# Early gate/up products over three weight blocks instead of two, with the third block's weight rows in an h block tile

## The chip, the core and the metric

The kernel runs on one core of a Trainium2 chip. Its time is the device time of one execution in microseconds (us). The names of the engines are TensorE (PE in the profile; PEld is its weight load), VectorE (DVE), ScalarE (ACT), GpSimd (POOL) and SyncE (SP, which here only issues transfers). Each engine works through its own list of instructions in the order in which the program holds them.

## The reference

One encoder layer on 1024 tokens of width 1024: a gated feed-forward network (FFN), a mixer, a second FFN, a last norm.

```python
def _swiglu(x, w_gate, w_up, w_down):
    return (jax.nn.silu(x @ w_gate) * (x @ w_up)) @ w_down
...
        h = _rmsnorm(x, ffn1_norm[l])
        x = x + 0.5 * _swiglu(h, ffn1_w_gate[l], ffn1_w_up[l], ffn1_w_down[l])
        h = _rmsnorm(x, mix_norm[l])
        z = h @ w_in[l]
...
        x = x + jnp.concatenate([y_a, y_b], axis=-1) @ w_out[l]
        h = _rmsnorm(x, ffn2_norm[l])
        x = x + 0.5 * _swiglu(h, ffn2_w_gate[l], ffn2_w_up[l], ffn2_w_down[l])
    return _rmsnorm(x, final_norm)
```

The inner width of an FFN is 2816, which is 22 column blocks of 128 for gate and 22 for up.

## The kernel before

**Products.** The change lies in `gate_up`, which computes gate and up of one FFN. It multiplies in the Winograd form of Strassen's scheme: a 2x2 arrangement of blocks takes seven products instead of eight. A block `b` is one pair of weight columns of gate (`g`) or of up (`u`); there are 22, in the order g, u, g, u. Each block has seven products, M = 1 to 7. Product M multiplies a weight block, or a sum of weight blocks, with one of seven token blocks: A11, A12, A22, which are parts of the normed input h, and S1 to S4, which are sums and differences of such parts (`A_OF`: 1 uses A11, 2 A12, 5 S1, 6 S2, 3 S4, 7 S3, 4 A22). Every operand is split into a high and a low half in a short float format (`split`: ScalarE casts the high half, VectorE subtracts to get the low half), and a product is high times high, high times low and low times high (`mm3`, L137 to L139) over four slices k: 12 matmuls of 128x128 by 512 columns.

**Tiles.** The high and low halves of the seven token blocks are 14 tiles of pool `big`, which holds 14 (`h_units`; A11h is the high half, A11l the low one). A block's weights arrive as two rows of 512 KB (`row`, L288; r0 holds the quarters for M 1 and 2, r1 the others, and in M 5, 6, 7 and 4 VectorE overwrites quarters with their differences, L299, L302, L305, L308). Rows take one of five buffers of pool `raw`; a split weight (`wu`) takes one of eight buffers of pool `unit`, which the product that reads it gives back.

**The start of an FFN.** A11 and A12 are made first. The other token blocks are made by `kinds`: s1 (norms of the second half of the tokens, L233, sums, L249, and S1's split), s2 (L254), s4 (L259), s3 (L264), a22 (a split only). `STAGES` says behind which step each is written in the program. The steps of before are: M 1 and M 2 for blocks 0, 1, 2; then 5, 6, 3, 7, 4 for blocks 0 and 1 in turn; then 5, 6, 3, 7 of block 2; and from block 3 on one block after the other, M 1 of the block, M 4 of the block ahead of it, M 2, 5, 6, 3, 7. Weights are written six steps ahead (`ahead=6`), and the evacuations of the first six steps wait for step 6 (`hold=6`): product 6, 7 and 4 add to the PSUM bank of product 1 (X), so the copy `m1` must have left the bank before product 6 writes it. A scheduler orders each engine's instructions from this program; the order is what the section on the change shows.

`gate_up` runs twice, for the first FFN from the start and for the second from about 1045 us.

Of the kernel before, what the change touches and what calls it, by code (L numbers as in the profile page):

```python
# [10 lines left out]
F32 = mybir.dt.float32  # L11
# [6 lines left out]
P = 128  # L18
D = 1024
S = 1024  # L20
T = 512
# [25 lines left out]
A_OF = {1: "A11", 2: "A12", 3: "S4", 4: "A22", 5: "S1", 6: "S2", 7: "S3"}  # L47
UNITS = ("A11", "A12", "A22", "S1", "S2", "S3", "S4")
GROUPS = ((0, 4), (4, 8), (8, 11))
STAGES = (5, 5, 6, 8, 9)  # L50


class Net:
# [219 lines left out]
    def gate_up(self, n):  # L273
        nc, d = self.nc, self.d
        self.actd = {
            (u, g): self.dp.tile([q1 - q0, P, T], F32, name=f"act{n}{u}{g}")
            for u in UNITS
            for g, (q0, q1) in enumerate(GROUPS)
        }
        blocks = [(p, m) for p in range(NP) for m in ("g", "u")]  # L280
        rows, sil, fence = {}, {}, {}
        early = 3

        def row(b, i):
            p, m = blocks[b]
            if (b, i) not in rows:
                rows[b, i] = self.rp.tile([P, 2, T], F32, tag="r", name=f"r{m}{i}")
                nc.sync.dma_start(rows[b, i].rearrange("p a t -> p (a t)"), d[f"{m}{n}"][2 * p + i])  # L288
            return rows[b, i]

        def weight(b, M):
            r0 = row(b, 0)
            if M in (1, 2):
                src = r0[:, M - 1]
            else:
                r1 = row(b, 1)
                if M == 5:
                    src = r1[:, 0]
                    nc.vector.tensor_sub(src, r1[:, 0], r0[:, 0])  # L299
                elif M == 6:  # L300
                    src = r1[:, 0]
                    nc.vector.tensor_sub(src, r1[:, 1], r1[:, 0])  # L302
                elif M == 7:
                    src = r0[:, 0]
                    nc.vector.tensor_sub(src, r1[:, 0], r0[:, 0])  # L305
                elif M == 4:
                    src = r0[:, 1]
                    nc.vector.tensor_sub(src, r0[:, 1], r1[:, 0])  # L308
                else:
                    src = r1[:, 1]  # L310
            w = self.unit("wu")
            name = self.split(w[:, 0], w[:, 1], src, after=fence.get("early"))
            if (b, M) == (early - 1, 2):
                fence["early"] = name
            return w

        bank, part = {}, {}
        place = {1: "X", 6: "X", 7: "X", 4: "X", 5: "Z", 3: "Z", 2: "W"}

        def product(b, M, w):  # L320
            ch = place[M]
            new = M in (1, 2, 5)
            if new:
                bank[b, ch] = self.fpsum("p" + ch)
            ps = bank[b, ch]
            hh, hl = self.h[A_OF[M]]
            ins = self.mm3(
                ps, [(w[:, 0, k * P : k * P + P], w[:, 1, k * P : k * P + P], hh[:, k], hl[:, k]) for k in range(4)], start=new
            )
            self.last_mm = ins.ins.name  # L330
            if (b, M) == (len(blocks) - 1, 1):
                self.gate = self.last_mm

        def evac(b, M):
            p, m = blocks[b]
            ps = bank[b, place[M]]
            key = {1: "m1", 5: "m5", 6: "u2"}.get(M)
            if key:
                part[b, key] = self.tmp(key)
                nc.scalar.copy(part[b, key], ps)  # L340
                return
            if M == 4:
                if m == "g":
                    s = self.tmp("s21")
                    self.table(s, ps, AF.Silu)
                    sil[p, "A21"] = s
                else:
                    s = sil[p, "A21"]
                    nc.vector.tensor_mul(s, ps, s)
                    finish(p)  # L350
                return
            key, name = {2: ("m1", "A11"), 3: ("u2", "A12"), 7: ("m5", "A22")}[M]
            t = part.pop((b, key))
            nc.vector.tensor_add(t, ps, t)
            if m == "g":
                self.table(t, t, AF.Silu)
                sil[p, name] = t
            else:
                s = sil[p, name]
                nc.vector.tensor_mul(s, t, s)  # L360
                store(p, name, s)

        def store(p, u, t):
            g = next(i for i, (q0, q1) in enumerate(GROUPS) if q0 <= p < q1)
            nc.sync.dma_start(self.actd[u, g][p - GROUPS[g][0]], t)

        def finish(p):
            a11, a12, a21, a22 = (sil.pop((p, q)) for q in ("A11", "A12", "A21", "A22"))
            s1 = a21
            nc.vector.tensor_add(s1, a21, a22)  # L370
            store(p, "S1", s1)
            s2, s3, s4 = (self.tmp(q) for q in ("S2", "S3", "S4"))
            nc.vector.tensor_sub(s2, s1, a11)
            store(p, "S2", s2)
            nc.vector.tensor_sub(s3, a22, s2)
            store(p, "S3", s3)
            nc.vector.tensor_sub(s4, a12, s2)
            store(p, "S4", s4)

        steps = [(b, M) for M in (1, 2) for b in range(early)]  # L380
        steps += [(b, M) for M in (5, 6, 3, 7, 4) for b in range(early - 1)]
        steps += [(early - 1, M) for M in (5, 6, 3, 7)]
        for b in range(early, len(blocks)):
            steps += [(b, 1), (b - 1, 4)] + [(b, M) for M in (2, 5, 6, 3, 7)]
        steps.append((len(blocks) - 1, 4))
        return steps, weight, product, evac
# [524 lines left out]
def layer(ctx, tc, d):  # L911
# [17 lines left out]
    with ExitStack() as f1:  # L929
# [6 lines left out]
        r[1] = net.rsqrt(ps)  # L936
        net.run(*net.gate_up(1), ahead=6, hold=6, stages=list(zip(STAGES, kinds)))

# [44 lines left out]
    with ExitStack() as f2:  # L983
# [6 lines left out]

        stages = [(1, stats2)] + list(zip(STAGES, h2[1]))
        net.run(*net.gate_up(2), ahead=6, hold=6, stages=stages)
# [85 lines left out]
```

## Time and profile before

| | |
|---|---|
| median of three runs | 1708.3 us (1707.48 to 1708.93) |
| the profiled execution | 1708.28 us, of which the span 1706.5 us |
| TensorE busy | 1655.5 us, 97% of the span |
| VectorE busy | 1111.5 us, 65% |
| ScalarE busy | 679.4 us, 40% |

The profile covers the span; 1.8 us of the execution lie around it. TensorE is busy nearly everywhere, so what is to be read are the stretches in which it is not, or in which its granted clock is below 1.00. A row of the timeline gives the start, the length, and in brackets the time that the engine stood idle ahead of it and what ended that. Matmuls and vector instructions overlap their neighbours, so the pace is read from start to start, not from the length.

### The profile page before, as it was taken

What the parts mean: (1) busy time and instruction counts of PE and PEld (TensorE: products, weight loads), DVE (VectorE), ACT (ScalarE), POOL (GpSimd) and SP (SyncE); (2) the same over time, 40 slices, a digit from 0 to 9 for tenths busy, and PEclk for the clock granted to TensorE, in tenths of its full rate; (3) what the DMA queues carried; (4) which work ended last, traced back from release to release, by engine and by line L of the source; (5) the groups of instructions that cost most, each with busy time, mean ns of one, the idle gap of its engine ahead of it and who ended that gap; (6) DMA issues with size and microseconds to landing.
All of it is one profiled execution on the core that took longest, in us unless ns stands there. A gap on an engine that the chain in (4) does not pass through costs nothing.

```text
span 1706.5 us, 19863 instructions
## 1 busy us (share of the span) xinstructions
PE 1655.5 (97%) x7314; PEld 1345.9 (79%) x7314; DVE 1111.5 (65%) x1771; ACT 679.4 (40%) x1155; POOL 60.3 (4%) x79
## 2 busy tenths in 40 slices
PE   6899999999999999999999999899999999999997
PEld 3688888888888877888877887688888888888875
DVE  7976556565569668852626538966666666579584
ACT  5633333333444445531423324533333333444452
POOL 0000000000000000110304300000000000000000
PEclk9999999999999999999999999999999999999999
DMA  4243232232695332230310342232323332793331
GB/s 161 70 141 100 98 105 99 96 108 75 239 331 188 117 112 74 74 88 19 98 46 13 117 142 86 88 123 93 105 99 105 105 111 75 257 319 133 108 121 50
DMA packets 95697, 200.07 MB, mean 117 GB/s; under 512 B 10472, under 2 KB 14568, under 8 KB 95600
## 3 DMA queue, kind: packets, MB, share of 16 engines
q1 hardware_dynamic: 89104, 187.21, 32.7%
q10 hardware_dynamic: 6496, 11.60, 1.9%
q8 instruction: 57, 0.93, 0.2%
q14 instruction: 40, 0.33, 0.1%
HBM read 145.78 MB, written 52.99 MB: 116 GB/s over the span
## 4 chain that ended last, share of the span: by engine, by line
PE 91%; DVE 7%; ACT 1%; DMA 0%; issue 0%; SPq 0%; DVEq 0%; ACTq 0%
PE pX L137 14%; PE pX L139 14%; PE pX L138 14%; PE pZ L138 7%; PE pZ L137 7%; PE pZ L139 7%; PE pW L139 3%; PE pW L138 3%; PE pW L137 3%; PE pg L139 3%; PE pg L137 3%; PE pg L138 3%; PE pt L583 2%; PE pt L582 2%; PE pt L584 2%; DVE x L233 1%
## 5 line engine op out<-in xcount | busy, mean ns | idle before, releaser
L206 ACT CAST au<-as 128x512 fp32r<-128x512 f32 x154 | 95.9, 623 | 208.7 <-PE pX L139 102.7
L209 DVE TENSOR_TENSOR au<-as,au 128x512 fp32r<-128x512 f32 x154 | 106.1, 689 | 107.7 <-ACT au L206 107.4
L209 DVE TENSOR_TENSOR wu<-rg,wu 128x512 fp32r<-128x512 f32 x154 | 106.1, 690 | 101.4 <-ACT wu L206 101.0
L206 ACT CAST wu<-ru 128x512 fp32r<-128x512 f32 x154 | 95.8, 622 | 155.3 <-PE pX L139 68.4
L209 DVE TENSOR_TENSOR wu<-ru,wu 128x512 fp32r<-128x512 f32 x154 | 105.7, 688 | 57.6 <-ACT wu L206 57.1
L137 PE MATMUL pX<-au,wu 128*128 128x512 f32 x352 | 137.2, 390 | 0.0
L138 PE MATMUL pX<-au,wu 128*128 128x512 f32 x352 | 137.0, 389 | 0.0
L139 PE MATMUL pX<-au,wu 128*128 128x512 f32 x352 | 136.9, 389 | 0.0
L206 ACT CAST wu<-rg 128x512 fp32r<-128x512 f32 x154 | 95.1, 621 | 103.1 <-issue 53.1
L209 DVE TENSOR_TENSOR wu<-wq,wu 128x512 fp32r<-128x512 f32 x154 | 105.2, 685 | 4.2 <-ACT wu L206 4.2
L206 ACT CAST wu<-wq 128x512 fp32r<-128x512 f32 x154 | 94.4, 616 | 8.3 <-PE pX L139 4.2
L137 PEld LDWEIGHTS pX<-au,wu 128*128 128x128 f32 x352 | 66.1, 188 | 14.4 <-ACT wu L206 0.7
L139 PEld LDWEIGHTS pX<-au,wu 128*128 128x128 f32 x352 | 66.1, 188 | 13.8
L138 PEld LDWEIGHTS pX<-au,wu 128*128 128x128 f32 x352 | 66.1, 188 | 13.6
L137 PE MATMUL pX<-A11h,wu 128*128 128x512 f32 x176 | 70.3, 400 | 4.6 <-ACT wu L206 3.4
L139 PE MATMUL pX<-A11h,wu 128*128 128x512 f32 x176 | 70.3, 400 | 3.9 <-DVE wu L209 3.9
L137 PE MATMUL pZ<-S1h,wu 128*128 128x512 f32 x176 | 68.1, 394 | 5.0 <-ACT wu L206 4.7
L138 PE MATMUL pZ<-S1l,wu 128*128 128x512 f32 x176 | 69.3, 394 | 2.6 <-DVE S1l L209 2.5
L137 PE MATMUL pX<-S3h,wu 128*128 128x512 f32 x176 | 68.9, 395 | 2.8 <-ACT S3h L206 2.8
L138 PE MATMUL pX<-A11l,wu 128*128 128x512 f32 x176 | 70.3, 399 | 0.2 <-DVE A11l L209 0.2
L137 PE MATMUL pX<-S2h,wu 128*128 128x512 f32 x176 | 68.6, 390 | 1.9 <-ACT m L340 1.9
L137 PE MATMUL pX<-A22h,wu 128*128 128x512 f32 x176 | 69.7, 396 | 0.0
(255 smaller groups left out, 4125.4 us busy)
## 6 DMA issues: line engine op xcount, KB each, us to landing
rg<-g SPq DMA_DIRECT2D x44, 512.0 KB, 3.5
ru<-u SPq DMA_DIRECT2D x44, 512.0 KB, 3.5
wq<-d SPq DMA_DIRECT2D x88, 256.0 KB, 5.4
x<-x SPq DMA_DIRECT2D x64, 256.0 KB, 5.3
as<-act1S SPq DMA_DIRECT2D x44, 256.0 KB, 3.6
as<-act2S SPq DMA_DIRECT2D x44, 256.0 KB, 3.2
act1S<-S SPq DMA_DIRECT2D x33, 256.0 KB, 2.1
as<-act1A SPq DMA_DIRECT2D x33, 256.0 KB, 4.9
```

Source lines behind the costliest of these rows:

```text
L137: nc.tensor.matmul(out, wh, hh, start=start and i == 0, stop=False, skip_group_check=True)
L138: nc.tensor.matmul(out, wh, hl, start=False, stop=False, skip_group_check=True)
L139: ins = nc.tensor.matmul(out, wl, hh, start=False, stop=stop and i == n - 1, skip_group_check=True)
L206: cast = nc.scalar.copy(hi, src)
L209: (eng or nc.vector).tensor_sub(lo, src, hi.bitcast(F32))
L233: nc.vector.scalar_tensor_tensor(x, x, g, r[c], op0=ALU.mult, op1=ALU.mult)
L582: nc.tensor.matmul(ps, hh, wh, start=k == 0, stop=False)
L583: nc.tensor.matmul(ps, hh, wl, start=False, stop=False)
L584: nc.tensor.matmul(ps, hl, wh, start=False, stop=k == KT - 1)
```

## The change

The third block (`early - 1`, block 2) takes part in all early rounds: the steps are 5, 6, 3, 7, 4 for blocks 0, 1 and 2 in turn, without the last (M 4 of block 2, which stands behind M 1 of block 3 as before). `STAGES` moves with the longer rounds. The two rows of block 2 no longer take buffers of pool `raw`; they share one tile of pool `big`.

```diff
-STAGES = (5, 5, 6, 8, 9)
+STAGES = (5, 5, 7, 10, 12)
...
-        rows, sil, fence = {}, {}, {}
+        rows, sil, fence, extra = {}, {}, {}, []
         early = 3
 
         def row(b, i):
             p, m = blocks[b]
             if (b, i) not in rows:
-                rows[b, i] = self.rp.tile([P, 2, T], F32, tag="r", name=f"r{m}{i}")
+                if b == early - 1:
+                    if not extra:
+                        extra.append(self.big.tile([P, 4, T], F32, tag="b", name=f"r{m}"))
+                    rows[b, i] = extra[0][:, 2 * i : 2 * i + 2]
+                else:
+                    rows[b, i] = self.rp.tile([P, 2, T], F32, tag="r", name=f"r{m}{i}")
...
         steps = [(b, M) for M in (1, 2) for b in range(early)]
-        steps += [(b, M) for M in (5, 6, 3, 7, 4) for b in range(early - 1)]
-        steps += [(early - 1, M) for M in (5, 6, 3, 7)]
+        steps += [(b, M) for M in (5, 6, 3, 7, 4) for b in range(early)][:-1]
```

All 14 tiles of `big` already hold a token block, so the shared tile comes to lie where A22l, the low half of A22, is put later: A22l is written when block 2's rows have been read for the last time. The numbers of matmuls, vector instructions, casts and transfers stay as they are; only their order at the start of the two FFNs differs, and line numbers behind the new lines are 4 or 5 higher.

ScalarE at the first FFN, where S1 is cast (`wu_373` and `wu_376` are the weights of the twelfth step; `x10` to `x13` are tokens of the second half). Before:

```order
L206 CAST wu_341<-ru1_304 128x512
L206 CAST wu_373<-ru1_304 128x512
L206 CAST S1h_187<-x10_118 128x512
L206 CAST S1h_187<-x11_120 128x512
L206 CAST S1h_187<-x12_122 128x512
```

With the change:

```order
L206 CAST wu_359<-ru1_304 128x512
L206 CAST wu_376<-rg_258 128x512
L206 CAST wu_426<-rg1_285 128x512
L206 CAST wu_457<-ru1_304 128x512
L206 CAST S1h_187<-x10_118 128x512
L206 CAST S1h_187<-x11_120 128x512
```

Two more weight casts, those of steps 13 and 14 (M 3 of blocks 0 and 1), stand ahead of S1's casts.

VectorE at the first FFN, where A22l is written (`wu_516` is M 4's weight of block 1; `rg_541` is the second row of block 2). Before:

```order
L308 TENSOR_TENSOR ru0_253<-ru0_253,ru1_304 128x512
L209 TENSOR_TENSOR S3l_192<-x13_124,S3h_191 128x512
L209 TENSOR_TENSOR A22l_186<-x14_126,A22h_185 128x512
L209 TENSOR_TENSOR wu_516<-ru0_253,wu_516 128x512
L209 TENSOR_TENSOR A22l_186<-x15_128,A22h_185 128x512
L209 TENSOR_TENSOR A22l_186<-x16_130,A22h_185 128x512
L209 TENSOR_TENSOR A22l_186<-x17_132,A22h_185 128x512
L354 TENSOR_TENSOR u2_483<-pZ_408,u2_483 128x512
L299 TENSOR_TENSOR rg1_541<-rg1_541,rg0_258 128x512
```

With the change (`rg_258` is the tile with both rows of block 2; `wu_635` is block 2's M 4, the last that reads it):

```order
L313 TENSOR_TENSOR rg_258<-rg_258 128x512
L359 TENSOR_TENSOR m5_455<-pX_291,m5_455 128x512
L209 TENSOR_TENSOR wu_653<-ru0_615,wu_653 128x512
L209 TENSOR_TENSOR wu_635<-rg_258,wu_635 128x512
L365 TENSOR_TENSOR m5_424<-m5_455,m5_424 128x512
L209 TENSOR_TENSOR A22l_186<-x14_126,A22h_185 128x512
L209 TENSOR_TENSOR A22l_186<-x15_128,A22h_185 128x512
```

A22l no longer follows S3l at once; block 2's weights come between them, `wu_635` as the last. Counted in the whole list, the first A22l row stands 50 rows behind the last S1l row here, against 34 before; in the second FFN 47 against 30.

TensorE at the first FFN, from S3 to A22 (`wu_544` is M 5's weight of block 2, `wu_486` M 4's of block 0). Before:

```order
L138 MATMUL pX_291<-S3l_192,wu_468 128x512
L139 MATMUL pX_291<-S3h_191,wu_468 128x512
L137 MATMUL pZ_649<-S1h_187,wu_544 128x512
L138 MATMUL pZ_649<-S1l_188,wu_544 128x512
L137 MATMUL pX_272<-A22h_185,wu_486 128x512
L138 MATMUL pX_272<-A22l_186,wu_486 128x512
L139 MATMUL pX_272<-A22h_185,wu_486 128x512
```

With the change (`wu_553` is M 7's weight of block 2, `wu_617` M 1's of block 3):

```order
L138 MATMUL pX_310<-S3l_192,wu_553 128x512
L139 MATMUL pX_310<-S3h_191,wu_553 128x512
L137 MATMUL pX_272<-A22h_185,wu_571 128x512
L137 MATMUL pX_291<-A22h_185,wu_598 128x512
L137 MATMUL pX_721<-A11h_181,wu_617 128x512
L138 MATMUL pX_721<-A11l_182,wu_617 128x512
L139 MATMUL pX_721<-A11h_181,wu_617 128x512
L138 MATMUL pX_272<-A22l_186,wu_571 128x512
```

Block 2's S1, S2, S4 and S3 products now lie ahead of A22, one in each round, and no weight of block 2 stands between S3 and A22.

## Rows read from the trace of the kernel before

**Rows 1.** The page: busy time of TensorE, and the last chain by engine.

```profile
PE 1655.5 (97%) x7314; PEld 1345.9 (79%) x7314; DVE 1111.5 (65%) x1771; ACT 679.4 (40%) x1155; POOL 60.3 (4%) x79
...
PE 91%; DVE 7%; ACT 1%; DMA 0%; issue 0%; SPq 0%; DVEq 0%; ACTq 0%
```

**Rows 2.** Busy time by stretch, first FFN (columns in the first row).

```profile
core 0: us, PE busy (x) PEld busy (x) DVE busy (x) ACT busy (x) POOL busy (x), PEclk, DMA share, GB/s
...
65.60:77.41 11.81, 7.69 (x25) 5.29 (x24) 11.81 (x21) 7.06 (x13) 0.00 (x0) 0.86 0.65 199
77.41:101.17 23.76, 23.76 (x97) 19.34 (x98) 20.29 (x33) 10.65 (x19) 0.00 (x0) 0.93 0.40 133
```

**Rows 3.** Timeline of TensorE, first FFN.

```profile
45.62 0.39 PE L137 MATMUL pZ<-S1h,wu 128*128 128x512 f32 x1
...
54.58 0.50 PE L137 MATMUL pX<-S2h,wu 128*128 128x512 f32 x1 [0.70 <-ACT m L340]
...
67.79 1.15 PE L137 MATMUL pX<-S3h,wu 128*128 128x512 f32 x2 [2.01 <-ACT S3h L206]
...
77.41 0.50 PE L137 MATMUL pZ<-S1h,wu 128*128 128x512 f32 x1 [2.10 <-ACT wu L206]
...
101.01 0.39 PE L137 MATMUL pW<-A12h,wu 128*128 128x512 f32 x1
...
103.73 0.39 PE L137 MATMUL pZ<-S1h,wu 128*128 128x512 f32 x1
```

**Rows 4.** Timeline of VectorE, first FFN.

```profile
35.34 0.68 DVE L299 TENSOR_TENSOR ru<-ru,ru 128x512 f32<-128x512 f32 x1
...
41.94 0.69 DVE L209 TENSOR_TENSOR wu<-ru,wu 128x512 fp32r<-128x512 f32 x1 [0.38 <-ACT wu L206]
...
51.95 0.68 DVE L209 TENSOR_TENSOR S1l<-x,S1h 128x512 fp32r<-128x512 f32 x1
...
72.43 0.68 DVE L209 TENSOR_TENSOR A22l<-x,A22h 128x512 fp32r<-128x512 f32 x1
```

**Rows 5.** Timeline of TensorE, second FFN.

```profile
1075.06 0.50 PE L137 MATMUL pX<-S2h,wu 128*128 128x512 f32 x1 [1.22 <-ACT m L340]
...
1087.14 0.73 PE L137 MATMUL pX<-S3h,wu 128*128 128x512 f32 x2 [0.83 <-ACT S3h L206]
...
1096.17 0.50 PE L137 MATMUL pZ<-S1h,wu 128*128 128x512 f32 x1 [2.59 <-ACT wu L206]
...
1118.20 0.39 PE L137 MATMUL pW<-A12h,wu 128*128 128x512 f32 x1
```

**Rows 6.** Timeline of ScalarE, second FFN.

```profile
1073.41 0.59 ACT L340 COPY m<-pZ 128x512 f32<-128x512 f32 x1 [0.77 <-PE pZ L139]
1073.90 0.62 ACT L206 CAST S2h<-x 128x512 fp32r<-128x512 f32 x1
1074.42 0.59 ACT L340 COPY m<-pX 128x512 f32<-128x512 f32 x1
```

**Rows 7.** Timeline of VectorE, second FFN.

```profile
1043.40 0.68 DVE L884 TENSOR_TENSOR x<-pg,x 128x512 f32<-128x512 f32 x1
...
1060.58 2.07 DVE L233 SCALAR_TENSOR_TENSOR x<-x,cols,rstd 128x512 f32<-128x512 f32 x3
...
1071.90 0.69 DVE L209 TENSOR_TENSOR S1l<-x,S1h 128x512 fp32r<-128x512 f32 x1
```

**Rows 8.** Busy time by stretch, second FFN, same columns.

```profile
1064.56:1075.06 10.50, 7.62 (x26) 3.78 (x24) 10.34 (x18) 4.75 (x9) 0.00 (x0) 1.00 0.00 0
...
1086.20:1096.17 9.97, 6.13 (x25) 4.29 (x24) 9.97 (x18) 6.13 (x12) 0.00 (x0) 1.00 0.51 161
```

**Rows 9.** Transfers issued by SyncE's queue, first FFN, then second.

```profile
65.96 0.33 SPq L288 DMA_DIRECT2D rg<-g  x1
...
1000.39 0.33 SPq L288 DMA_DIRECT2D rg<-g  x1
```

## The prediction

> **What bounds the kernel.** The page says first where to look: TensorE is busy 97% of the span and makes up 91% of the chain that ended last, VectorE 7% of it [rows 1]. So the time is TensorE's list of matmuls plus the moments in which it stands still or has a lower clock, and this change can only act on the latter, since it removes no instruction. The stretches give those moments at the start of the first FFN: from 65.60 to 77.41 TensorE is busy 7.69 of 11.81 us while VectorE is busy all of it, and the granted clock, 1.00 elsewhere, is 0.86 there and 0.93 behind it, means of the two levels of 2.4 and 1.2 GHz [rows 2]. The timeline of TensorE shows the two large waits: 2.01 us ahead of S3's products, and 2.10 us ahead of block 2's first product with S1, for a weight [rows 3]. The second FFN has the same two places, 0.83 and 2.59 us [rows 5], and its S1 stage is paced by VectorE as well, 7.62 busy of 10.50 [rows 8].
>
> Why it waits is read from VectorE's list. It is full from S1 on: 34 rows lie between the last S1l row (51.95) and the first A22l row (72.43), so 0.602 us per row with nothing left over [rows 4]. In two-block rounds TensorE gets 24 matmuls per token block. Their pace, from 101.01 to 103.73 for 12, is 0.2267 us each, so a round is 5.44 us [rows 3]; VectorE's list has 11 rows for S4 and 15 for S3 in that time (differences, low halves, the round's weights, evacuations), 6.6 and 9.0 us. TensorE catches up at S3 and stops. Then block 2 adds a stop of its own: its second weight row can only be fetched at 65.96, when a buffer of the five comes free [rows 9], and its first weight stands behind A22l on VectorE, and ahead of A22's products on TensorE.
>
> **What is to be won.** I measure from the first S2 product to the first M 2 product of block 3. In both orders 14 products, 168 matmuls, lie between: 168 x 0.2267 = 38.1 us without a wait. Before, the first FFN takes 101.01 - 54.58 = 46.4 us [rows 3], a loss of 8.3; the second 1118.20 - 1075.06 = 43.1 [rows 5], a loss of 5.0. The 8.3 are the waits of 2.01 and 2.10, the lower clock, (1 - 0.86) x 11.81 = 1.65 and (1 - 0.93) x 23.76 = 1.66 [rows 2], and 0.9 of small waits. If nothing waited the gain would be 13.3 us; that is the outer bound on one side.
>
> **What is added: S1 comes later, first FFN.** VectorE's list is the same to the second L299 row, 35.34, which ends its turn at 35.94 [rows 4]. Then the change has nine rows of weights to the split of the twelfth step, which starts in both orders when its cast is done, 41.94 [rows 4], since that cast waits for the same product. From there, five norms and two other rows to the first S1l row. A norm is 0.66: 41.94 to 51.95 is 16 rows, six of them norms, and (10.01 - 10 x 0.602) / 6 = 0.66 [rows 4]. That gives 41.94 + 5 x 0.66 + 2 x 0.602 = 46.4. But on ScalarE the casts of steps 13 and 14 now stand ahead of S1's. The fourteenth weight takes the buffer of the sixth, which comes free with the last M 2 product at 45.62 [rows 3]. A cast has a pace of 0.5 (1073.90 to 1074.42 in the second FFN) [rows 6]; two of them end at 46.7, so the first S1l row starts at 46.8. Twelve rows to the last one, three of them norms, are 7.4: 54.2, against 51.95.
>
> S2's products then wait for the copy `m1`. In the first FFN of before this is 54.58 - 51.95 = 2.6 behind the last S1l row, in the second 1075.06 - 1071.90 = 3.2 [rows 5, 7]; the difference is one S2h cast between the two copies on ScalarE [rows 6], and the change has that cast there in both FFNs. So S2 starts at 57.4, 2.8 us later than before.
>
> **Then nothing should wait.** To the end of S3 TensorE has 120 matmuls, 27.2 us, so it reaches A22's low half, five matmuls further, at 57.4 + 28.3 = 85.7. VectorE has 50 rows from the last S1l row to the first A22l row: 54.2 + 30.1 = 84.3, done at 85.0. This is the tight place, 0.7 us of cover, and without it the wait grows one for one. S3l lies 18 rows ahead of A22l, about 11 us, and is not late; three-block rounds give TensorE 8.16 us each. Block 2's rows no longer wait for a buffer and are fetched at the start. So M 2 of block 3 starts at 57.4 + 38.1 = 95.5; I add 0.3 for small waits, 95.8. Against 101.01 the first FFN gains 5.2.
>
> **Second FFN.** From 1043.40, behind the last A12l row, to the first norm at 1060.58 VectorE took 17.2 us for 26 rows [rows 7], which are 15.5 by count, so 1.7 of waits. The change has 29 rows there, 17.3 by count: if they fill the waits, no delay; if the waits stay, 1.8. I take 0.9. From that norm to the last S1l row the list is unchanged, so S2 starts at 1076.0 and M 2 of block 3 at 1114.1, a gain of 4.1 (3.2 to 5.0). A22l there is 47 rows behind S1l, 28.3: 1072.8 + 28.3 = 1101.1, done at 1101.8, and TensorE needs it at 1103.4, 1.6 of cover.
>
> **Edits at nothing.** The shared tile delays A22l, priced above by the rows ahead of it. The two rows of block 2 in one tile are the same two transfers; in the second FFN they go ahead of the first row, which was sent at 1000.39 [rows 9], some 45 us before use. All other lists are unchanged beyond the two starts.
>
> **Sum.** 1708.28 - 5.2 - 4.1 = 1699.0 us for the profiled execution; its 1708.28 and the median of 1708.3 are the same, so 1699.0 is for the median too. The change has more small gaps in a row than the first FFN of before, and what they do to the clock is the largest open cost.
>
> **Rivals.** *The clock falls in the gaps.* The change has a gap of about 1.2 us ahead of S1, small ones within it (2.9 of 10.50 us are idle in the S1 stage of the second FFN [rows 8]) and about 1.3 ahead of S2. For it: gaps of 2.01 and 2.10 were followed by 0.86 and 0.93 [rows 2, 3]. Against it: the second FFN has such a row of gaps, ending with 1.22, at a clock of 1.00 throughout [rows 5, 8], and 2.59 cost nothing there either, so length alone does not decide. One fall costs 1.65; one in each FFN gives 1702.3, two in each 1705.6. The Trainium skill, "TensorE: Matmul & The Clock Gate", section "A second HAM failure mode: psum-queue depth-cycling", says that short idle moments between groups of matmuls, with PSUM banks being cycled, make the clock swing between its two levels. By that rule this rival would be the likeliest; the row at 1064.56 with its clock of 1.00 does not bear it out.
>
> *A22l is late: slower.* It is written after block 2's last weight, so whatever delays that weight stops TensorE at A22. Say VectorE's list slips by s in each FFN beyond the count. The waits are s - 0.7 and s - 1.6, and past some 2 us each also costs 1.65 of clock. Even at 2s + 1.0 = 9.3, s = 4.2, nothing is gained; at s = 6 the time is 1699.0 + 5.3 + 4.4 + 3.3 = 1712. For it: 16 and 17 more rows stand ahead of A22l, and each may wait for a cast or an evacuation. Against it: over the same stretch of before VectorE lost nothing in 34 rows [rows 4], and the 22nd weight's buffer comes free 10 us earlier. A slip of 2 is plausible (1.7 were lost in the second FFN's start), which gives 1.3 + 0.4: 1700.7.
>
> *The gain is given back.* Block 3 and those behind it could find their weights late, because VectorE does block 2's share earlier and block 3's later. Then TensorE, up to 9.3 us ahead, waits for weights until VectorE is where it was: 1708. Against it: VectorE is idle 3.5 of the 23.76 us behind 77.41 [rows 2], so it has room.
>
> **Chances.** Forecast, 1697 to 1701: 0.60. Clock, 1701 to 1705.6: 0.20. A22l slipping by some 2 to 4: 0.08, of which half ends below 1704.9. Given back: 0.07. Slower: 0.05. A measurement of this kernel tells about 0.2%, 3.4 us, from no change. Faster by more, below 1704.9: 0.60 + 0.19 + 0.05 + 0.04 (a partial give-back) = 0.88; same 0.08; slower 0.04. The range, 1695.8 to 1704, holds the forecast, one fall of the clock in each FFN and an A22l slip, and below it 3 us of the outer bound of 1695.0, which is 13.3 less than before.
>
> **What would show it.** S2's first product near 57.4 and, with the first gain taken off, near 1070.8; no wait over 0.5 ahead of S3; M 2 of block 3 near 95.8 and 1108.9; a clock of 1.00 from S2 on. Wrong would be: a wait at A22 for A22l of more than 1 us, a clock under 0.95 between S1 and A22, or waits for weights in blocks 3 and 4.

## The result, and the profile after

The changed kernel takes 1697.67 us in the median of six runs (1696.97 to 1698.85), the kernel before, in six runs on the same chip, 1707.44 (1705.82 to 1708.93). The ratio is 0.9944, with a 95% interval of 0.9931 to 0.9957: 9.8 us, or 0.56%, faster. The forecast was 1699.0 us, in a range of 1695.8 to 1704.0. The profiled execution took 1697.15 us, of which the span is 1695.4, against 1706.5 before.

The page of the changed kernel has the same counts of instructions as [rows 1]; TensorE's busy time is 5.6 us less:

```profile
PE 1649.9 (97%) x7314; PEld 1343.9 (79%) x7314; DVE 1110.3 (65%) x1771; ACT 679.3 (40%) x1155; POOL 60.6 (4%) x79
```

Not all of that is the clock. Under "The sum" below, equal work is compared: 500 matmuls of each kernel, counted from the same one on. Over these, TensorE's busy time falls by 3.2 us in the first FFN, where the lower clock of before had cost 3.3 [rows 2], and by 1.1 us in the second, where the mean clock is 1.00 in both kernels and only the stops are fewer. The rest lies outside these stretches.

The stretches of both FFNs, columns as in [rows 2]: the first row is the S1 stage, the next ones go from S2's first product on.

```profile
46.61:57.16 10.55, 7.71 (x25) 3.88 (x25) 10.40 (x17) 4.75 (x9) 0.00 (x0) 1.00 0.00 1
57.16:68.10 10.94, 10.94 (x48) 9.09 (x49) 10.90 (x19) 9.03 (x16) 0.00 (x0) 1.00 0.06 24
68.10:84.49 16.39, 16.39 (x74) 13.55 (x73) 16.32 (x28) 10.99 (x20) 0.00 (x0) 1.00 0.39 119
84.49:95.30 10.81, 10.81 (x49) 8.98 (x48) 10.20 (x18) 4.09 (x7) 0.00 (x0) 1.00 0.22 85
95.30:140.00 44.70, 44.70 (x199) 37.02 (x198) 30.85 (x49) 17.97 (x31) 0.00 (x0) 1.00 0.41 136
...
1069.22:1096.60 27.38, 27.38 (x121) 22.68 (x122) 27.24 (x46) 20.28 (x36) 0.00 (x0) 1.00 0.29 97
1096.60:1107.30 10.70, 10.70 (x49) 8.87 (x48) 10.70 (x19) 4.73 (x8) 0.00 (x0) 1.00 0.27 77
```

From S2 on TensorE is busy in every microsecond of these stretches, at a clock of 1.00. Before, the like stretches had 7.69 of 11.81 us at 0.86, then 0.93 [rows 2], and 6.13 of 9.97 [rows 8]. VectorE is as full as it was, 16.32 of 16.39 us: it is no faster, it is only no longer waited for.

The timeline of TensorE in the changed kernel, first FFN and then second:

```profile
46.61 0.73 PE L137 MATMUL pZ<-S1h,wu 128*128 128x512 f32 x2 [1.28 <-ACT S1h L206]
...
53.59 0.73 PE L137 MATMUL pZ<-S1h,wu 128*128 128x512 f32 x2
54.75 0.50 PE L138 MATMUL pZ<-S1l,wu 128*128 128x512 f32 x1 [0.42 <-DVE S1l L209]
...
57.16 0.50 PE L137 MATMUL pX<-S2h,wu 128*128 128x512 f32 x1 [1.22 <-ACT m L345]
...
85.62 0.39 PE L138 MATMUL pX<-A22l,wu 128*128 128x512 f32 x1
...
95.37 0.39 PE L137 MATMUL pW<-A12h,wu 128*128 128x512 f32 x1
...
1039.67 0.50 PE L137 MATMUL pX<-A11h,wu 128*128 128x512 f32 x1 [3.36 <-ACT wu L206]
...
1069.22 0.50 PE L137 MATMUL pX<-S2h,wu 128*128 128x512 f32 x1 [1.22 <-ACT m L345]
...
1096.78 0.39 PE L138 MATMUL pX<-A22l,wu 128*128 128x512 f32 x1
...
1107.43 0.39 PE L137 MATMUL pW<-A12h,wu 128*128 128x512 f32 x1
```

S2 starts 2.58 us later than before, at 57.16, and M 2 of block 3 still comes 5.64 us earlier, at 95.37 against 101.01 [rows 3] (5.2 of it over equal work, see below). In the second FFN M 2 of block 3 is 10.77 us earlier, 1107.43 against 1118.20 [rows 5]. VectorE's list, in the same order, shows the last S1l rows and the A22l rows:

```profile
54.01 0.68 DVE L209 TENSOR_TENSOR S1l<-x,S1h 128x512 fp32r<-128x512 f32 x1
...
84.60 2.49 DVE L209 TENSOR_TENSOR A22l<-x,A22h 128x512 fp32r<-128x512 f32 x4
...
1066.07 0.68 DVE L209 TENSOR_TENSOR S1l<-x,S1h 128x512 fp32r<-128x512 f32 x1
...
1094.93 2.49 DVE L209 TENSOR_TENSOR A22l<-x,A22h 128x512 fp32r<-128x512 f32 x4
```

### The profile page after: what moved, and what is told of

Read it like the earlier page. It is cut to its first block, busy times and chain, and to the rows that moved or that the text cites. A ratio compares the mean times of both kernels' runs of the same rounds, so it can differ in the third digit from the quotient of the medians.

```text
span 1695.4 us, 19873 instructions
## 1 busy us (share of the span) xinstructions
PE 1649.9 (97%) x7314; PEld 1343.9 (79%) x7314; DVE 1110.3 (65%) x1771; ACT 679.3 (40%) x1155; POOL 60.6 (4%) x79
## 4 chain that ended last, share of the span: by engine, by line
PE 93%; DVE 5%; ACT 1%; DMA 1%; issue 0%; SPq 0%; DVEq 0%; ACTq 0%
PE pX L137 14%; PE pX L139 14%; PE pX L138 14%; PE pZ L138 7%; PE pZ L139 7%; PE pZ L137 7%; PE pW L137 3%; PE pW L138 3%; PE pW L139 3%; PE pg L139 3%; PE pg L137 3%; PE pg L138 3%; PE pt L587 2%; PE pt L586 2%; PE pt L588 2%; DVE x L233 1%
## 5 line engine op out<-in xcount | busy, mean ns | idle before, releaser
L206 ACT CAST au<-as 128x512 fp32r<-128x512 f32 x154 | 95.8, 622 | 206.9 <-PE pX L139 104.5
L209 DVE TENSOR_TENSOR wu<-rg,wu 128x512 fp32r<-128x512 f32 x154 | 106.1, 690 | 95.8 <-ACT wu L206 95.4
L139 PEld LDWEIGHTS pX<-au,wu 128*128 128x128 f32 x352 | 66.1, 188 | 13.7
L138 PEld LDWEIGHTS pX<-au,wu 128*128 128x128 f32 x352 | 66.1, 188 | 13.7
L137 PE MATMUL pW<-A12h,wu 128*128 128x512 f32 x176 | 69.2, 393 | 0.0
L138 PE MATMUL pW<-A12l,wu 128*128 128x512 f32 x176 | 69.2, 393 | 0.0
```

The source lines that it names most:

```text
L137: nc.tensor.matmul(out, wh, hh, start=start and i == 0, stop=False, skip_group_check=True)
L138: nc.tensor.matmul(out, wh, hl, start=False, stop=False, skip_group_check=True)
L139: ins = nc.tensor.matmul(out, wl, hh, start=False, stop=stop and i == n - 1, skip_group_check=True)
L206: cast = nc.scalar.copy(hi, src)
L209: (eng or nc.vector).tensor_sub(lo, src, hi.bitcast(F32))
```

## The experiments

Theory: rounds of three blocks give TensorE more matmuls for each row that VectorE makes, so that the wait at S3 and the lower clock behind it go, and the early rows of block 2 take away the wait for its weight. The rivals: the early rows alone do it; a late A22l stops TensorE; the gain is given back. The measurements of one group share the runs of the kernel before: a median of 1708.0 us for the first four experiments, 1707.43 for the other four.

### The shared tile alone

```diff
-STAGES = (5, 5, 7, 10, 12)
+STAGES = (5, 5, 6, 8, 9)
...
-        steps += [(b, M) for M in (5, 6, 3, 7, 4) for b in range(early)][:-1]
+        steps += [(b, M) for M in (5, 6, 3, 7, 4) for b in range(early - 1)]
+        steps += [(early - 1, M) for M in (5, 6, 3, 7)]
```

> The shared tile for block 2's rows alone; products and stages stay in the order of before (two-block rounds for S1, S2, S4, S3, A22, then block 2's own). Theory, three-block rounds pay: the tile only takes away the second large wait of each FFN (2.10 us and 2.59 us ahead of block 2) and the lower clock behind the first of them (1.66 us), 6.4 us in all, so about 1701.0 us; the wait ahead of S3's products (2.01 and 0.83 us) and the lower clock near it stay in the trace, and block 2's first product starts without a wait. Rival, the early rows are the whole gain and the rounds give nothing: 1697.7 us, the changed kernel's time, with no wait above 0.5 us ahead of S3. Second rival, without the rounds VectorE has no earlier room for block 2's weights and the early rows are worth nothing: 1706 us or more, with the wait for block 2's weight still there.

It took 1701.91 us, ratio 0.9968 (0.9956 to 0.9981): 6.1 us faster than before. TensorE's timeline and the stretch around S3, of this kernel:

```profile
67.10 1.14 PE L137 MATMUL pX<-S3h,wu 128*128 128x512 f32 x2 [2.03 <-ACT S3h L206]
74.49 0.39 PE L137 MATMUL pZ<-S1h,wu 128*128 128x512 f32 x1
```

```profile
64.90:77.00 12.10, 10.05 (x35) 7.21 (x35) 12.10 (x21) 8.98 (x16) 0.00 (x0) 0.86 0.62 197
```

Block 2's first product starts at 74.49 without a wait, and the wait of 2.03 us at S3 stays, with a clock of 0.86: (1 - 0.86) x 12.10 = 1.7 us. The whole change is 1701.91 - 1697.67 = 4.2 us faster than this kernel in the medians, and over equal work in the two traces (the table under "The sum" below) 3.0 us in the first FFN and 1.9 in the second. The 3.0 are less than the wait and the clock together, 3.7, because S2 starts earlier in this kernel: 9.8 us behind the last matmul of M 2 (44.11 to 53.89), against 12.2 with the change (44.94 to 57.16). So the tile gives five to six tenths of the gain, and the rounds on top of it the rest. That the tile gives all of it, or nothing, is excluded; the rounds without the tile were not run. One expected row was missed: the 0.83 us at S3 of the second FFN did not come back, only the 0.42 for S3l behind it.

It is not the transfer that the tile saves TensorE from. In the second FFN of before, block 2's second row was sent at 1058.43, and VectorE first read it at 1094.79 (first two lines). A row lands 3.5 us after its issue, by the median of the page, and VectorE was busy from 1086.20 on without a gap [rows 8]. In the first FFN the row was sent at 65.96 [rows 9] and first read at 76.04. With the tile VectorE makes the same difference at 1040.87 (last line), long ahead of A22l, which starts at 1098.25.

```profile
1058.43 0.33 SPq L288 DMA_DIRECT2D rg<-g  x1
...
1094.79 0.68 DVE L299 TENSOR_TENSOR rg<-rg,rg 128x512 f32<-128x512 f32 x1
```

```profile
1040.87 0.68 DVE L304 TENSOR_TENSOR rg<-rg 128x512 f32<-128x512 f32 x1
```

So the wait was for a weight that stood late on VectorE's list, behind A22l. The tile changes both the time at which the row is asked for and the place of A22l, which must now come behind block 2's weights; no run separates which of the two moved the weights forward on the list.

### The stages of before

The edit is the first of the two above, alone: the table of stages stays (5, 5, 6, 8, 9) with the new rows and rounds.

> The whole change but for the table of stages, which stays (5, 5, 6, 8, 9): the splits of S4, S3 and A22 come earlier on VectorE's list, ahead of weights of the rounds that run then. Theory, TensorE is now 10 us and more behind VectorE's rows at all places but A22l, so who of them comes first costs nothing: 1697.7 us, within 1.0. Rival, the new steps in the table carry a part of the gain, since a split that stands ahead of a weight delays it: a wait for a weight of 1 us or more in the S2 or S4 round of each FFN, and 1699.7 to 1702 us.

1698.31 us, ratio 0.9946 (0.9933 to 0.9958), the same as the changed kernel within what is measured. The waits of TensorE in both FFNs are those of the changed kernel, and no wait for a weight is among them in the S2 and S4 rounds. Over equal work both FFNs take what they take in the changed kernel, within 0.05 us. The table of stages carries nothing.

### The change in the first FFN alone

```diff
-                if b == early - 1:
+                if n == 1 and b == early - 1:
```

In the same way the second FFN has the steps and the stages of before.

> The change in the first FFN alone; the second FFN has the rows, the order and the stages of before. Theory, the two gains are separate and add up: the first FFN gives 5.2 to 5.8 us and the second nothing, so 1701.6 to 1702.2 us; block 3's first M 2 product near 95.4, and in the second FFN the waits of 0.83 us (S3) and 2.59 us (block 2's weight) are back. Rival, the gain of one FFN is given back in the stages that follow it, so that a single FFN's change is worth less than half: 1704 us or more.

1702.82 us, ratio 0.997 (0.996 to 0.9981): 5.2 us faster than the 1708.0 of its group, the lower end of the expected 5.2 to 5.8, though the time is 0.6 us above the expected 1702.2. The second FFN shows the waits of [rows 5] again:

```profile
1079.07 0.73 PE L138 MATMUL pX<-S3h,wu 128*128 128x512 f32 x2 [0.83 <-ACT S3h L207]
...
1088.11 0.50 PE L138 MATMUL pZ<-S1h,wu 128*128 128x512 f32 x1 [2.54 <-ACT wu L207]
```

Over equal work the first FFN takes what it takes in the changed kernel (120.15 against 120.02 us) and the second what it took before (123.40 against 123.45). The gains of the two FFNs add up, and nothing of the first is lost in the thousand microseconds behind it.

### Copies of M 1 not held back

```diff
-            if i < hold:
+            if i < hold and M != 1:
```

> The changed kernel, but the copies of M 1's sums out of PSUM are no longer held back until the sixth product, so they stand ahead of the S1 and S2 casts on ScalarE and free their banks early; no work is added or removed. Theory, the tight place decides: the wait of 1.22 us ahead of S2's products goes in each FFN, S2 starts 1.2 us earlier, but A22l is written when it was, and its cover of 0.3 and 0.8 us is used up, so 0.9 and 0.4 us come back as a wait at A22: a gain of 0.3 to 1.2 us, about 1696.9 us, with a wait for A22l in the trace. Rival, the freed banks let products of S2 fill the small waits of the S1 stage as well, and other products fill the wait at A22: the gain is 2.4 us or more, up to 5 (1692.7 to 1695.3 us).

1692.12 us, ratio 0.9909 (0.9895 to 0.9922): 15.9 us faster than before and 5.5 less than the changed kernel. This is the best of all kernels here, and my theory of it was wrong. TensorE's timeline in this kernel:

```profile
52.66 0.50 PE L138 MATMUL pZ<-S1l,wu 128*128 128x512 f32 x1 [0.48 <-DVE S1l L209]
...
53.70 0.62 PE L137 MATMUL pX<-S2h,wu 128*128 128x512 f32 x2
54.16 0.62 PE L137 MATMUL pZ<-S1h,wu 128*128 128x512 f32 x2
...
82.80 0.39 PE L138 MATMUL pX<-A11l,wu 128*128 128x512 f32 x1
...
85.75 0.39 PE L138 MATMUL pX<-A22l,wu 128*128 128x512 f32 x1
```

The waits left between 45 and 106 us are 1.3 for S1h and 1.0 for S1l. In the changed kernel the fourth slice of the S1 stage, from 53.59 to S2's start at 57.16, took 3.57 us for six matmuls, which at the pace of 0.2267 are 1.36, a loss of 2.2, or 4.4 in both FFNs. Here the banks are free, and the scheduler puts products with S2 into that slice. At A22 it puts block 3's products with A11 ahead of A22l's matmuls, so the tight place does not stop TensorE. Over equal work this kernel is 2.5 us faster than the changed one in the first FFN and 2.6 in the second, 5.1 in all. That is 0.7 more than the two losses; I have no row for that rest.

### Eight and sixteen rows ahead of A22l

```diff
+            x = self.x
+            for _ in range(8):
+                pad = self.st.tile([P, T], F32, tag="s", name="late")
+                nc.vector.tensor_add(pad, x[0][0], x[0][1])
             for k, q in enumerate(quads()):
                 put("A22", k, q[3])
```

> The changed kernel with eight more rows on VectorE right ahead of the splits of A22 in each FFN (sums that nothing uses; the result stays the same). At 0.602 us each A22l comes 4.8 us later. Theory of the prediction, the cover is 0.3 and 0.8 us and past it the wait grows one for one: 4.5 and 4.0 us, with perhaps 1.65 of clock: 1706 to 1709 us, with a wait for A22l of some 4 us in each FFN. Rival, the scheduler has other products at hand there (block 3's first product with A11, 12 matmuls of 0.2267 us, 2.7 us, and more behind it) and puts them ahead of the low half's matmuls: 1697.7 to 1700 us, with no wait or one below 1.5 us.

> The same with sixteen rows, 9.6 us for A22l in each FFN; the result stays the same. Theory of one for one: waits of 9.3 and 8.8 us, 1715.8 us or more. Rival, other products fill some 3 to 5 us of each and the rest is waited for: waits of 3 to 6 us in each FFN, 1705 to 1711 us. From this and the run with eight rows the true cover can be read: what the sixteen rows cost less than 9.6 in each FFN.

With eight rows: 1697.08 us, ratio 0.9937 (0.9923 to 0.9951), no cost in the median; over equal work the first FFN is 0.45 us longer than in the changed kernel and the second the same. VectorE's A22l starts at 88.73, 4.1 us later than in the changed kernel, and TensorE has no wait in that place:

```profile
77.31 4.31 DVE L271 TENSOR_TENSOR late<-x,x 128x512 f32<-128x512 f32 x7
88.73 2.51 DVE L209 TENSOR_TENSOR A22l<-x,A22h 128x512 fp32r<-128x512 f32 x4
```

```profile
84.10 0.39 PE L137 MATMUL pX<-A11h,wu 128*128 128x512 f32 x1
...
89.98 0.39 PE L138 MATMUL pX<-A22l,wu 128*128 128x512 f32 x1
```

Block 3's products with A11 and A12 now stand ahead of A22l's, which moves from 85.62 to 89.98. With sixteen rows: 1710.12 us, ratio 1.0013 (1.0004 to 1.0022), 12.4 us more than the changed kernel. Its TensorE waits, first FFN and second, and the stretches behind the two waits:

```profile
PE pX L139 <- DVE wu L209: 4.9, 1, 4.9
...
PE pX L139 <- DVE wu L209: 3.5, 1, 3.5
```

```profile
90.00:95.42 5.42, 5.42 (x13) 3.94 (x13) 5.42 (x10) 1.23 (x2) 0.00 (x0) 0.51 0.61 232
...
1108.00:1112.00 4.00, 3.82 (x9) 2.39 (x10) 4.00 (x7) 1.22 (x2) 0.00 (x0) 0.64 0.68 260
```

The sixteen rows are 9.6 us, and 4.9 and 3.5 of them are waited for: 4.7 and 6.1 us in the two FFNs are covered. Behind the first wait the granted clock is 0.51, near the lower of the two levels, for 5.42 us, which costs (1 - 0.51) x 5.42 = 2.7 us; behind the second it is 0.64 for 4.00 us, 1.4. Waits and clock, 12.5 us, are close to the 12.4 by which the median grew; over equal work the two traces differ by 13.7, so 1.2 us there have no row. It is not A22l that is waited for but a weight of block 3 that stands behind the added rows on VectorE.

### The kernel before with copies of M 1 not held back

The edit is the one above, in the kernel before.

> The kernel before, with the copies of M 1's sums not held back (the one line that made the changed kernel faster by 5.5 us). Theory, in two-block rounds TensorE stops at S3 for VectorE, whose list is not made shorter by this: the wait of 0.70 and 1.22 us ahead of S2 goes, and the waits ahead of S3 grow by as much, to 2.5 to 2.9 and about 2.0 us; nothing is gained, 1707.4 us within 1.5. Rival, what the line gives does not depend on the order of products: 5 us here too, 1702.5 us.

1707.06 us, ratio 0.9995 (0.9986 to 1.0004): no gain. TensorE's timeline in this kernel:

```profile
51.30 0.50 PE L137 MATMUL pX<-S2h,wu 128*128 128x512 f32 x1 [0.36 <-ACT S2h L206]
...
65.85 0.74 PE L137 MATMUL pX<-S3h,wu 128*128 128x512 f32 x2 [2.10 <-ACT S3h L206]
...
76.08 0.79 PE L137 MATMUL pZ<-S1h,wu 128*128 128x512 f32 x1 [2.76 <-ACT wu L206]
...
1084.68 0.73 PE L137 MATMUL pX<-S3h,wu 128*128 128x512 f32 x2 [2.55 <-ACT S3h L206]
...
1093.72 0.50 PE L137 MATMUL pZ<-S1h,wu 128*128 128x512 f32 x1 [0.99 <-ACT wu L206]
```

```profile
76.08:99.48 23.40, 23.40 (x96) 19.24 (x97) 20.30 (x33) 10.63 (x19) 0.00 (x0) 0.93 0.43 140
```

S2 starts earlier and what it wins is waited for later: in the first FFN mostly at block 2's weight (2.76 against 2.10 before), not at S3 as I had expected; in the second at S3 (2.55 against 0.83). From S1 to block 2's first product the recorded waits add up to 7.1 us in the first FFN, against 5.9 before, and to 5.0 in the second, against 6.5: 12.1 against 12.4 us in all. The clock covers this up in each FFN: in the first it costs (1 - 0.93) x 23.40 = 1.6 us, against 3.3 before [rows 2], and in the second 1.7 (the row of 1084.68 in the last section), against nothing. Over equal work the first FFN is 0.3 us longer and the second 0.65 shorter. So that nothing is gained is shown for the two FFNs together; in the second alone the waits became 1.5 us shorter, and the clock hid more than half of that. The same line is worth 5.5 us once the rounds hold three blocks.

### Three-block rounds for S1 and S2 alone

```diff
-        steps += [(b, M) for M in (5, 6, 3, 7, 4) for b in range(early)][:-1]
+        steps += [(b, M) for M in (5, 6) for b in range(early)]
+        steps += [(b, M) for M in (3, 7) for b in range(early - 1)]
+        steps += [(early - 1, M) for M in (3, 7)]
+        steps += [(b, 4) for b in range(early - 1)]
```

> The changed kernel with three-block rounds for S1 and S2 alone; S4 and S3 run over two blocks, then block 2's S4 and S3 products, then A22 for two blocks. Theory, what counts is how much TensorE has been given ahead of S3: two more products (24 matmuls, 5.4 us) stand there against a wait of 2.0 us, so two rounds of the five are enough: 1697.7 us within 1.5, and no wait ahead of S3. Rival, every round of three pays by itself: with two rounds of four that TensorE can use up, half of the 3.5 us that the rounds give over the tile alone is lost, so 1699.5 to 1701.9 us, with a wait at S3 or at A22.

1698.38 us, ratio 0.9945 (0.9933 to 0.9958), 0.7 us from the changed kernel, which is within the spread of either; over equal work the two are the same within 0.03 us. From S2's start TensorE does not stop:

```profile
59.26:97.00 37.74, 37.74 (x166) 31.28 (x167) 36.89 (x63) 24.14 (x42) 0.00 (x0) 1.00 0.24 80
```

Two more products ahead of S3 are enough; the rounds for S4, S3 and A22 add nothing that can be measured.

## Why the prediction was right

**What bounds.** The reading holds: TensorE stopped because its two-block rounds need less time than VectorE's rows for them. Undoing the rounds brings the wait at S3 back (2.03 us, the tile alone), and freeing TensorE earlier without them gives nothing over the two FFNs (the kernel before with the copies not held). Two readings of the prediction were not right. It gave two reasons for block 2's stop, the late fetch of its second row and the place of its first weight behind A22l; TensorE waited for the place, when the row was already there (the shared tile alone). And the clock of before is not 1.00 elsewhere: it is 0.87 from 20.00 to 45.62, and 0.92 from 1045.68 to 1066.00, behind a wait of 3.35 us that the forecast left out and the change does not touch.

**First FFN, 5.2 forecast, 5.64 in the trace.** The last S1l row was put at 54.2 and came at 54.01; S2 at 57.4, and came at 57.16; M 2 of block 3 at 95.8, and came at 95.37. From S2 on, 38.21 us passed against 38.1 by count, so the 0.3 for small waits were 0.1. The single-FFN kernel gave 5.2 us. The absolute times agree in part by luck: the last matmul of M 2, ahead of all that is forecast here, starts at 45.39 in the trace of before and at 44.94 in that of the change, and in the other kernels with three-block rounds at 43.32 to 47.04. Counted from there M 2 of block 3 comes 55.62 us later before and 50.43 with the change: 5.2, as forecast.

**Second FFN, 4.1 forecast, 4.76 in the trace.** From the first product with A11 to M 2 of block 3 the changed kernel takes 1107.43 - 1039.67 = 67.76 us. Before, it was 72.52 (1118.20, less a start at 1045.68 in that trace). The step that was mis-sized is the delay of S2: 0.9 was taken between 0 and 1.8. The last S1l row comes 28.68 us behind the first row after A12l (1066.07 less 1037.39, where that row stands in the changed kernel), against 28.50 before [rows 7], so the delay is 0.2: the added weights fill waits that were there.

**The sum.** 5.64 and 4.76, and 0.4 for a shorter wait in the work between the FFNs (0.93 us against 1.38, for a low half), are the 10.77 by which M 2 of block 3 is earlier in the second FFN. The spans differ by 11.1 and the medians by 9.8. What the change does shows without the chance of the start when equal work is compared: from the start of the last matmul of M 2 of block 2 to the start of the 500th matmul behind it. Before, then with the change, first FFN and second each, columns as in [rows 2] (one or two more matmuls reach in at the edges):

```profile
45.39:170.59 125.20, 119.14 (x501) 95.14 (x500) 96.66 (x154) 57.31 (x98) 0.00 (x0) 0.97 0.32 106
1063.88:1187.33 123.45, 116.72 (x501) 92.86 (x500) 95.96 (x154) 55.69 (x98) 0.00 (x0) 1.00 0.31 102
```

```profile
44.94:164.96 120.02, 115.91 (x502) 93.17 (x500) 96.93 (x155) 57.06 (x98) 0.00 (x0) 1.00 0.31 101
1057.91:1176.57 118.66, 115.63 (x502) 93.26 (x500) 93.88 (x151) 56.12 (x98) 0.00 (x0) 1.00 0.30 102
```

The same comparison for every kernel, in us:

| kernel | first FFN | second FFN |
|---|---|---|
| before | 125.20 | 123.45 |
| the change | 120.02 | 118.66 |
| the shared tile alone | 123.02 | 120.60 |
| the stages of before | 120.06 | 118.64 |
| the change in the first FFN alone | 120.15 | 123.40 |
| copies of M 1 not held back | 117.54 | 116.03 |
| eight rows ahead of A22l | 120.47 | 118.66 |
| sixteen rows | 127.80 | 124.61 |
| before, copies of M 1 not held back | 125.52 | 122.80 |
| three-block rounds for S1 and S2 alone | 120.04 | 118.63 |

The gains are 5.2 and 4.8 us, 10.0 in all, against 5.2 and 4.1 forecast and 9.8 in the medians. The first was right, and the second is off by the 0.7 of S2's delay.

**The clock.** The rival with a chance of 0.20 did not come. The changed kernel has the row of gaps that it needs, 1.28 ahead of S1, 0.54, 0.47 and 0.42 in it, and 1.22 behind it, and the granted clock is 1.00 in the stretch of the gaps and in those shown behind it. The second FFN has such a row too, 0.19, 0.54, 0.48, 0.42 and 1.22, in a stretch at 1.00:

```profile
1058.00:1069.22 11.22, 8.19 (x29) 4.26 (x27) 11.07 (x19) 5.49 (x11) 0.00 (x0) 1.00 0.00 0
```

By the Trainium skill, "TensorE: Matmul & The Clock Gate", section "A second HAM failure mode: psum-queue depth-cycling", short idle moments between groups of matmuls while banks are cycled make the clock swing between its levels. Five gaps of 0.2 to 1.3 us within 11 us did not do that here, in either FFN; whether more of them in a row would is not shown.

**A22l, the step that was wrong.** "Without it the wait grows one for one" was not so. The row came at 84.60, done at 85.28 for a matmul at 85.62: the cover was 0.34 us, 0.7 forecast, and tight as said. In the second FFN it was 1.2 (done at 1095.62 for a matmul at 1096.78), against 1.6 forecast and the 0.8 that the expectations above took. But 4.8 us more of rows cost 0.45 us in the first FFN and nothing in the second, and 9.6 us brought waits of 4.9 and 3.5. The scheduler has block 3's products to put there, which my count left out. The slower rival, which stood on this price, was thus further off than I put it. What is shown holds for rows that the scheduler knows of; whether a row that comes late by chance would stop TensorE after 0.34 us was not tried.

**Given back.** It was not: from 95.30 to 140 TensorE is busy throughout in the changed kernel.

## What to carry to other kernels

Where two engines feed each other in rounds, compare the time of a round on each: the one that needs less stops at the end of a few rounds, and starting it earlier is worth nothing (0.4 us here, within the noise) until its rounds are longer (5.5 us then). Make longer only the rounds ahead of the stop; two of five did it here. And count a place as tight only after looking for other work that the scheduler may put there: 0.34 us of cover turned out to be 4.7 and more. Take a gain from two traces over equal work: the same product started up to 3.7 us apart (43.32 and 47.04) in kernels that do the same products up to it.

## What the runs showed of the chip that was not expected

The length of a gap on TensorE does not by itself tell whether the clock falls behind it. In the second FFN of the kernel before, the wait of 2.59 us [rows 5] is followed by 22.03 us at 1.00, and in that of the kernel before with the copies not held, 2.55 us is followed by 8.32 us at 0.79:

```profile
1096.17:1118.20 22.03, 22.02 (x97) 18.05 (x97) 20.11 (x33) 10.85 (x19) 0.00 (x0) 1.00 0.44 144
```

```profile
1084.68:1093.00 8.32, 7.62 (x24) 5.53 (x24) 8.32 (x15) 4.74 (x9) 0.00 (x0) 0.79 0.45 162
```

Why the one fell and the other did not stays open; no run here separates the length of the gap from what stood ahead of it. The wait of 3.36 us at the start of the second FFN, which no kernel here takes away, is followed by a mean of 0.92 over the next 20.33 us in the changed kernel:

```profile
1039.67:1060.00 20.33, 20.01 (x79) 15.76 (x80) 20.24 (x35) 9.59 (x18) 0.00 (x0) 0.92 0.20 75
```

That is (1 - 0.92) x 20.33 = 1.6 us beside the wait, and so the next place to look at.
